# A decoder layer with 32 experts on one core: when the engines read what TensorE has multiplied

## The chip, the cores and the metric

The kernel runs on one core of a Trainium2 chip. The core has five engines with an instruction queue each: TensorE (PE; its weight loads are shown apart as PEld), VectorE (DVE), ScalarE (ACT), GpSimd (POOL) and SyncE (SP), which here issues nearly all transfers; 16 DMA engines move the data. The metric is the time of one execution on the device in microseconds (us); less is better.

## The reference, cut to what matters

One layer: attention in two head groups, then a mixture of experts (each of 512 tokens goes to 4 of 32 experts), then a gated embedding and a last normalisation. The part that the change touches is the mixture:

```
def expert_block(args):            # xs: the tokens of one expert
    e, xs = args
    hh = jnp.dot(xs, w_gu[e]) + b_gu[e]            # 1024 -> 2 x 1024
    glu, lin = jnp.split(hh, 2, axis=-1)
    glu = jnp.minimum(glu, SWIGLU_LIMIT)
    lin = jnp.clip(lin, -SWIGLU_LIMIT, SWIGLU_LIMIT)
    act = glu * jax.nn.sigmoid(SWIGLU_ALPHA * glu) * (lin + 1.0)
    return jnp.dot(act, w_dn[e]) + b_dn[e]         # 1024 -> 1024
...
yr = yb.reshape(n_rows, d) * row_gate[:, None].astype(yb.dtype)
y = jax.ops.segment_sum(yr, row_tok, num_segments=t + 1)[:t]
```

All 32 experts have 8 MB + 4 MB of float32 weights each, and each weight is used once.

## The kernel before

After attention and routing (about the first 345 us) the experts are sorted by how many tokens they have and worked off in 26 **runs**: 20 runs of one expert, with room for 128 tokens down to 72, and 6 runs of two experts with room for 64 tokens each (**pairs**). An expert's weights come in 12 **pieces** of 1 MB: eight "u" pieces (`w_gu`: u0 to u3 the glu half, u4 to u7 the linear half) and four "d" pieces (`w_dn`). A run multiplies its own u pieces and, between them, the d pieces of the run before it, in the order that `phase` writes out (line 48).

Each piece goes through three stages. SP loads it into one of 8 buffers (`RAW`, line 776). Then it is **split**: ACT writes its high half as float16 (`hl`, line 219), DVE what is left of it (line 220), into one of 6 buffers (`HL`). Then TensorE multiplies it in three passes (`mm3`, lines 225 to 227; `down_t`, lines 1357 to 1359). The d pieces of a pair are not split: TensorE reads them as float32 straight from `RAW`. A `RAW` buffer is free again after the split (or after the matmuls that read it), an `HL` buffer after the matmuls. `take(j)` emits the splits up to four pieces ahead of the piece j that it hands out (`AHEAD = 4`, `advance`).

ACT and DVE also read what TensorE has multiplied, out of PSUM banks:

- `gather` (line 1235) picks the tokens of the next run by matmuls with a one-hot matrix `oh`: four banks of `xT` (ACT, line 1250), the gates (DVE, lines 1259 and 1263) and the transposed one-hots `ohT` (ACT, line 1268). It is emitted whole after piece u5.
- `glu_of` after u3 (DVE line 1273, ACT line 1274) and `act_of` after u7 (DVE lines 1280 and 1281), then the split of the result, `acts`.
- `down_t` copies its transposed result `yT` (ACT, `yt`, line 1364) after the last d piece, TensorE turns it back into `y`; `y_out` multiplies it with the gate (ACT `yh`, line 1432; DVE `yl`, line 1433).
- `combine` adds three runs' results to the tokens: eight sums of six matmuls (line 1444), each added to `acc` by DVE (line 1446). `step()` emits one sum after each half of a u piece.

The small matmul results share two PSUM banks (`pg`), the halves of the u product four (`ph`), the d product two (`py`).

What sets the order: the code only emits; a list scheduler then orders each engine's queue by order of emission and by when it thinks that an instruction's operands are there. So an instruction emitted later may stand earlier. `behind(i, j)` (line 135) keeps i behind j on their engine, without a semaphore. Before, nothing in the experts' part is tied in that way. Once built, the order of a queue is fixed.

Of the kernel before, what the change touches and what calls it, by code (L numbers as in the profile page):

```python
# [9 lines left out]
F32 = mybir.dt.float32  # L10
# [45 lines left out]
def hybrid_layer(ctx: ExitStack, tc: tile.TileContext, x, p, positions, w_in, g_attn, g_cq, w_uq, g_ckv,  # L56
# [746 lines left out]
    def advance(upto):  # L803
# [3 lines left out]
        while nsp <= min(upto, len(jobs) - 1):  # L807
            j = jobs[nsp]
            if not native(j):
# [7 lines left out]
                else:  # L817
# [4 lines left out]
                    else:  # L822
                        hl(t[:, :2048], t[:, 2048:], RAW[:, f], SW)
# [401 lines left out]

    def onehots(pos, c, n=1):
# [8 lines left out]
    def gather(oh, gate, c, n=1, parts=True, mid=None):  # L1235

        if parts:
            xT = mp.tile([P, 2, KD, P], F16, name="xT", tag="xT", bufs=2)
        else:
            xT = mp.tile([P, KD, P], F32, name="xTf", tag="xT", bufs=2)  # L1240
        for h in range(2 if parts else 1):
            us = (uhl[h],) if parts else uhl
            for q in range(2):
                ps = pg()
                for k in range(4):
                    for j, u_ in enumerate(us):
                        for i in range(NT):
                            PE.matmul(ps[:, k * c:(k + 1) * c], u_[:, i, (q * 4 + k) * P:(q * 4 + k + 1) * P],  # L1248
                                      oh[:, i, :c], start=i == 0 and j == 0, stop=i == NT - 1 and j == len(us) - 1)
                A.activation((xT[:, h] if parts else xT)[:, q * 4:(q + 1) * 4, :c],  # L1250
                             ps[:, :4 * c].rearrange("p (k c) -> p k c", k=4), AF.Copy, scale=1.0 if parts else SW)
# [5 lines left out]
        gcl = mp.tile([P, 1], F32, name="gcl", bufs=3)  # L1257
        t4 = mp.tile([P, 4], F32, name="t4", bufs=2)
        V.tensor_scalar(t4[:c, :2 * n], ps[:c, 0:2 * n], 1.0 / (SX * SW), None, op0=OP.mult)
        w = c // n  # L1260
        for a in range(n):
            r = slice(a * w, (a + 1) * w)
            V.tensor_tensor(gcl[r], t4[r, a:a + 1], t4[r, n + a:n + a + 1], op=OP.add)
# [3 lines left out]
        ohT = mp.tile([P, SEQ], F16, name="ohT", bufs=5)  # L1267
        A.activation(ohT[:c], tp[:c, :SEQ], AF.Copy)
        return xT, gcl, ohT

    def glu_of(h, n):
        t = mp.tile([P, 512], F32, name="glu", bufs=2)[:, :n]
        V.tensor_scalar(t, h[:, :n], 1.0 / S, 7.0, op0=OP.mult, op1=OP.min)  # L1273
        A.activation(t, t, AF.Gelu_apprx_sigmoid)  # L1274
        return t

    def act_of(h, n, glu):

        t = mp.tile([P, 512], F32, name="ln", bufs=2)[:, :n]
        V.tensor_scalar(t, h[:, :n], 7.0 * S, -7.0 * S, op0=OP.min, op1=OP.max)  # L1280
        V.scalar_tensor_tensor(t, t, S, glu, op0=OP.add, op1=OP.mult)
        return t


    def up(get, put, xT, brow, c, acts):
# [4 lines left out]
        for a in range(2):  # L1290
# [6 lines left out]
            for q in range(4):  # L1297
                slot, w = get(4 * a + q)
                for m in range(2):
# [7 lines left out]
                    step()  # L1307
                put(4 * a + q)
                if q == 3:
                    if a:  # L1310
                        for j, h in enumerate(ps):
                            acts[j] = act_of(h, n, acts[j]).rearrange("p (m c) -> p m c", c=c)
                    else:
                        acts.extend(glu_of(h, n) for h in ps)
                yield

    def act_parts(acts, c):
        t = mp.tile([P, 2, 2, 4, P], F16, name="acts", tag="acts", bufs=1)
        r = [[t[:, j, b, :, :c] for b in range(2)] for j in range(2)]
# [393 lines left out]
```

## Time and profile before

| | us |
|---|---|
| three runs | 1547.34, 1550.41, 1550.46; median 1550.41 |
| the profiled execution | 1548.82 |
| its span, first to last instruction | 1546.7 |
| experts, from the trace | about 345 to 1455 |

The profile lists busy time by engine and stretch, groups of instructions by source line, who waited for whom, and the instructions in order of time. "Busy" of DVE and ACT is the union of their instructions; what is missing to the length of a stretch is idle. The mean granted clock of TensorE is 0.967 of full.

### The profile page before, as it was taken

To read this page: it belongs to the slowest core of one execution; us is meant where nothing else is said; L and a number is where in the kernel's file an instruction comes from. 1 tells how busy PE (TensorE), PEld (TensorE's weight loads), DVE (VectorE), ACT (ScalarE), POOL (GpSimd) and SP (SyncE) were. 2 spreads that over 40 slices of the span, in tenths; PEclk is the share of its full clock that TensorE was granted. 3 is DMA by queue.
4 is the path that set the end of the run, shared out by engine and by line. 5 is a ranking of instruction groups with operands and counts; after the bars stand their busy time and mean duration, and the time that the engine had idled before them with its cause. 6 is when DMAs were issued, how large, how long until landed. Compare 5 with 4: busy or idle time off the path is not lost. (4 is left out here: it accounts for less than half of the span.)

```text
span 1546.7 us, 41528 instructions
## 1 busy us (share of the span) xinstructions
PE 1366.5 (88%) x18126; PEld 981.7 (63%) x18126; DVE 1216.1 (79%) x1356; ACT 1012.6 (65%) x1168; POOL 49.6 (3%) x114
## 2 busy tenths in 40 slices
PE   7999899779989999999999899889889788798587
PEld 4766556475446686467885558868544777674257
DVE  7447876689874899849999669999884898989734
ACT  6458766558463677647777557777853786896534
POOL 2001000310000000000000000000000000000002
PEclk9999999879989999999999999999999999999799
DMA  7122131159999899969999879999996999899711
GB/s 254 41 86 83 56 110 30 54 204 380 355 371 362 320 394 358 345 243 400 404 339 359 328 291 408 383 361 346 341 394 229 375 406 367 285 377 350 282 69 56
DMA packets 124235, 432.81 MB, mean 280 GB/s; under 512 B 7977, under 2 KB 18770, under 8 KB 123986
## 3 DMA queue, kind: packets, MB, share of 16 engines
q1 hardware_dynamic: 123858, 429.85, 75.1%
q8 instruction: 144, 2.36, 0.6%
q14 instruction: 41, 0.34, 0.1%
q10 hardware_dynamic: 192, 0.26, 0.1%
HBM read 427.99 MB, written 2.10 MB: 278 GB/s over the span
## 5 line engine op out<-in xcount | busy, mean ns | idle before, releaser
L220 DVE SCALAR_TENSOR_TENSOR hl<-raw,hl 128x2048 f16<-128x2048 f32 x337 | 762.7, 2286 | 88.6 <-ACT hl L219 87.1
L219 ACT ACTIVATE hl<-raw 128x2048 f16<-128x2048 f32 x337 | 627.0, 1903 | 30.3 <-DMA raw<-in_w_gu_dram 11.1
L227 PE MATMUL hps<-xT,hl 128*128 128x80 f16 (+4 forms) x2560 | 339.2, 208 | 31.3 <-DVE hl L220 29.2
L225 PE MATMUL hps<-xT,hl 128*128 128x80 f16 (+4 forms) x2560 | 351.9, 208 | 3.2 <-ACT hl L219 3.0
L226 PE MATMUL hps<-xT,hl 128*128 128x80 f16 (+4 forms) x2560 | 351.2, 208 | 0.7 <-issue 0.7
L227 PEld LDWEIGHTS <-hl 128*128 128x128 f16 (+1 forms) x2672 | 257.8, 99 | 58.6 <-DVE hl L220 41.6
L225 PEld LDWEIGHTS <-hl 128*128 128x128 f16 (+1 forms) x2672 | 262.0, 99 | 28.2 <-issue 7.9
L226 PEld LDWEIGHTS <-hl 128*128 128x128 f16 (+1 forms) x2672 | 262.3, 99 | 16.9 <-issue 4.5
L1386 PE MATMUL hps<-hl,xT 128*64 128x512 f16 x1152 | 166.7, 404 | 38.8 <-DVE hl L220 30.8
L1386 PEld LDWEIGHTS <-xT 128*64 128x64 f16 x1152 | 77.9, 115 | 112.7 <-issue 73.5
L1358 PE MATMUL yT<-acts,hl 128*128 128x80 f16 (+3 forms) x960 | 122.4, 205 | 7.9 <-DVE acts L220 6.2
L1357 PE MATMUL yT<-acts,hl 128*128 128x80 f16 (+3 forms) x960 | 123.6, 205 | 4.2 <-issue 2.4
L1359 PE MATMUL yT<-acts,hl 128*128 128x80 f16 (+3 forms) x960 | 117.6, 205 | 9.4 <-DVE hl L220 7.8
L1250 ACT ACTIVATE xT<-pg 128x512 f16<-128x512 f32 (+4 forms) x104 | 51.5, 514 | 96.1 <-PE pg L1248 86.7
L1386 PE MATMUL y<-raw,actT 128*64 128x512 f32 x384 | 108.2, 603 | 0.0
L1359 PEld LDWEIGHTS <-hl 128*128 128x128 f16 x960 | 93.1, 100 | 20.5 <-DVE hl L220 11.2
L1357 PEld LDWEIGHTS <-hl 128*128 128x128 f16 x960 | 94.1, 100 | 11.4 <-issue 8.5
L1444 PE MATMUL pg<-yh,ohT 128*128 128x512 f16 (+4 forms) x208 | 81.9, 395 | 19.6 <-DVE acc L1446 13.2
L1358 PEld LDWEIGHTS <-hl 128*128 128x128 f16 x960 | 94.8, 100 | 3.2 <-issue 2.2
L1444 PE MATMUL pg<-yl,ohT 128*128 128x512 f16 (+4 forms) x208 | 81.4, 394 | 0.7 <-DVE yl L1433 0.6
L1444 PEld LDWEIGHTS <-ohT 128*128 128x128 f16 (+4 forms) x416 | 38.2, 100 | 67.9 <-issue 39.1
L1274 ACT ACTIVATE glu<-glu 128x512 f32<-128x512 f32 (+4 forms) x52 | 27.6, 550 | 70.3 <-DVE glu L1273 70.2
(376 smaller groups left out, 2339.1 us busy)
## 6 DMA issues: line engine op xcount, KB each, us to landing
raw<-in_w_gu_dram SPq DMA_DIRECT2D x256, 1024.0 KB, 8.4
raw<-in_w_dn_dram SPq DMA_DIRECT2D x128, 1024.0 KB, 8.7
raw<-in_w_in_dram SPq DMA_DIRECT2D x2, 2048.0 KB
raw<-in_w_o_dram SPq DMA_DIRECT2D x2, 2048.0 KB
raw<-in_w_ple_gate_dram SPq DMA_DIRECT2D x4, 1024.0 KB
acc<-in_x_dram SPq DMA_DIRECT2D x4, 512.0 KB, 3.6
raw<-in_w_in_dram SPq DMA_DIRECT2D x4, 512.0 KB, 7.1
out_dram<-acc SPq DMA_DIRECT2D x8, 256.0 KB, 2.4
```

What stands on the lines that cost most here:

```text
L219: later["hl"] = (A.activation(hi, src, AF.Copy, scale=scale), V.scalar_tensor_tensor(lo, src, scale, hi, op0=OP.mult, op1=OP.subtract))
L220: V.scalar_tensor_tensor(lo, src, scale, hi, op0=OP.mult, op1=OP.subtract))
L225: PE.matmul(ps, ah, bh, start=first, stop=False, skip_group_check=True)
L226: PE.matmul(ps, ah, bl, start=False, stop=False, skip_group_check=True)
L227: PE.matmul(ps, al, bh, start=False, stop=last, skip_group_check=True)
L1250: A.activation((xT[:, h] if parts else xT)[:, q * 4:(q + 1) * 4, :c], ps[:, :4 * c].rearrange("p (k c) -> p k c", k=4), AF.Copy, scale=1.0 ...
L1274: A.activation(t, t, AF.Gelu_apprx_sigmoid)
L1357: PE.matmul(o[f], w[0][:, m, r], ah, start=first and f % 4 == 0, stop=False, skip_group_check=True)
L1358: PE.matmul(o[f], w[0][:, m, r], al, start=False, stop=False, skip_group_check=True)
L1359: PE.matmul(o[f], w[1][:, m, r], ah, start=False, stop=last, skip_group_check=True)
L1386: PE.matmul(ps[n][E2[e]], xT[:, k, E2[e]] if whole else xT[:, a, k, E2[e]], (ws[e][1] if whole else ws[e][1][b])[:, m, c], start=not opene ...
L1444: PE.matmul(ps, ohT[:c, i * P:(i + 1) * P], y_[:c, n * 512:(n + 1) * 512], start=e == 0 and q == 0, stop=e == last and q == 1)
```

## The change

Five things change, all in the experts' part; every engine has as many instructions as before.

1. Results of TensorE are no longer read where they are emitted. The reading is put on a list by `after`, together with the last split emitted by then, and `flush` emits it, each instruction tied `behind` that split on its own engine. For the products of weights (`glus`, `acts_of`, `act_parts`, `yt`) `flush` follows at once after the piece; for gather, gates, sums and `y_out` it follows after the next piece.
2. `gather` is a generator of three steps (first half of `xT`, second half, gates and `ohT`), one step after each piece from d2 on.
3. `step` deals out two sums after each piece, d pieces too, instead of one after each half of a u piece, where no gather step is due.
4. The first d piece stands after u2 instead of u1, the second after u3.
5. The head and the tail get the calls of `flush` that this needs.

```diff
-    return [u[0], u[1], d[0], u[2], d[1], u[3], u[4], d[2], u[5], d[3], u[6], u[7]] if u and d else u + d
+    return [u[0], u[1], u[2], d[0], u[3], d[1], u[4], d[2], u[5], d[3], u[6], u[7]] if u and d else u + d
...
-                        hl(t[:, :2048], t[:, 2048:], RAW[:, f], SW)
+                        later["split"] = hl(t[:, :2048], t[:, 2048:], RAW[:, f], SW)
...
+    due = []
+
+    def after(f):
+        due.append((f, later.get("split")))
+
+    def flush():
+        while due:
+            f, sp = due.pop(0)
+            for i in f():
+                if sp is not None:
+                    behind(i, sp[0 if i.ins.engine == sp[0].ins.engine else 1])
+
+    def inline(steps):
+        for _ in steps:
+            flush()
...
+        def bank(us, o, q, scale):
+            ps = pg()
+            for k in range(4):
+                for j, u_ in enumerate(us):
+                    for i in range(NT):
+                        PE.matmul(ps[:, k * c:(k + 1) * c], u_[:, i, (q * 4 + k) * P:(q * 4 + k + 1) * P],
+                                  oh[:, i, :c], start=i == 0 and j == 0, stop=i == NT - 1 and j == len(us) - 1)
+            after(lambda: [A.activation(o[:, q * 4:(q + 1) * 4, :c], ps[:, :4 * c].rearrange("p (k c) -> p k c", k=4),
+                                        AF.Copy, scale=scale)])
...
             if mid is not None and not h:
+                flush()
                 mid()
+            yield
...
+        def gates():
+            t4 = mp.tile([P, 4], F32, name="t4", bufs=2)
+            yield V.tensor_scalar(t4[:c, :2 * n], ps[:c, 0:2 * n], 1.0 / (SX * SW), None, op0=OP.mult)
+            for a in range(n):
+                q = slice(a * w, (a + 1) * w)
+                yield V.tensor_tensor(gcl[q], t4[q, a:a + 1], t4[q, n + a:n + a + 1], op=OP.add)
+
+        after(gates)
...
+        after(lambda: [A.activation(ohT[:c], tp[:c, :SEQ], AF.Copy)])
+        yield
+
+    def glus(ps, n, r):
+
+        def first():
+            for h in ps:
+                r.append(mp.tile([P, 512], F32, name="glu", bufs=2)[:, :n])
+                yield V.tensor_scalar(r[-1], h[:, :n], 1.0 / S, 7.0, op0=OP.mult, op1=OP.min)
+            after(lambda: [A.activation(t, t, AF.Gelu_apprx_sigmoid) for t in r])
+
+        after(first)
+
+    def acts_of(ps, n, r, then):
+
+        def f():
+            for j, h in enumerate(ps):
+                t = mp.tile([P, 512], F32, name="ln", bufs=2)[:, :n]
+                yield V.tensor_scalar(t, h[:, :n], 7.0 * S, -7.0 * S, op0=OP.min, op1=OP.max)
+                yield V.scalar_tensor_tensor(t, t, S, r[j], op0=OP.add, op1=OP.mult)
+                r[j] = t
+            then()
+
+        after(f)
...
-                    step()
                 put(4 * a + q)
                 if q == 3:
                     if a:
-                        for j, h in enumerate(ps):
-                            acts[j] = act_of(h, n, acts[j]).rearrange("p (m c) -> p m c", c=c)
+                        acts_of(ps, n, acts, lambda: then(acts, c))
                     else:
-                        acts.extend(glu_of(h, n) for h in ps)
+                        glus(ps, n, acts)
                 yield
...
-                for n in range(2):
-                    A.activation(yt[n], ps[n][:, :4 * c], AF.Copy)
+                after(lambda: [A.activation(yt[n], ps[n][:, :4 * c], AF.Copy) for n in range(2)])
...
-                V.scalar_tensor_tensor(acc[:, i, n * 512:(n + 1) * 512], ps, 1.0 / SX,
-                                       acc[:, i, n * 512:(n + 1) * 512], op0=OP.mult, op1=OP.add)
+                a_ = acc[:, i, n * 512:(n + 1) * 512]
+                after(lambda ps=ps, a_=a_: [V.scalar_tensor_tensor(a_, ps, 1.0 / SX, a_, op0=OP.mult, op1=OP.add)])
                 yield 1
 
     sums = []
 
-    def step(n=1):
-
+    def step(n=2):
...
+        def f():
+            for n in range(2):
+                s_ = slice(n * 512, (n + 1) * 512)
+                yield A.activation(yh[:c, s_], y[n][:c], AF.Copy, scale=gcl[:c])
+                yield V.scalar_tensor_tensor(yl[:c, s_], y[n][:c], gcl[:c], yh[:c, s_], op0=OP.mult, op1=OP.subtract)
+
+        after(f)
         return yh, yl
...
             if u_ == "u":
                 next(g_up)
+                flush()
                 if q == 0 and turned_:
                     prev[2] = turn2(prev[2])
+                    continue
                 if q == 3:
                     at(ns_, 1)
+                if q == 4:
+                    at(ns_, 2)
+                    flush()
+                    step(99)
+                    if ns_ < LAST:
+                        nxt = []
+                        g_prep = prep(RUNS[ns_ + 1], nxt)
+                    continue
                 if q == 6 and g_down is not None:
                     next(g_down)
                     ended()
                     g_down = None
-                if q == 5:
-                    at(ns_, 2)
-                    if ns_ < LAST:
-                        step(99)
-                        nxt = prep(RUNS[ns_ + 1])
+                if g_prep is not None:
+                    next(g_prep, None)
+                else:
+                    step()
                 continue
             if q == 0:
                 ps_ = RUNS[prev[0]]
                 if not now:
                     prev[2] = turn2(prev[2])
+                    flush()
                 g_down = (down2 if len(ps_) > 1 else down if prev[1] == P else down_t)(
                     *access(ps_), prev[2], *(() if len(ps_) > 1 else (prev[1],)), prev[5])
             next(g_down)
-            if q == 3 and prev[5]:
+            flush()
+            if q == 3 and prev[5] and len(prev[5]) == 2 and (len(ps_) > 1 or prev[1] == P):
                 ended()
                 g_down = None
-        if now and len(us) == 1:
-            acts = act_parts(acts, c)
+            if g_prep is not None:
+                next(g_prep, None)
+            else:
+                step()
```

Two places in the queues. The first is **ACT** in a run of 80 tokens late in the expert part, from its reading of the glu half (`glu`) to that of the result (`yh`); `hl<-raw` is the split of a piece, `xT` and `ohT` the gather for the next run, `yt` the copy of the transposed result. Before:

```order
L1268 ACTIVATE ohT_17955<-ohT_ps_17950 80x512
L219 ACTIVATE hl_83<-raw_82 128x2048 x4
L1274 ACTIVATE glu_17697<-glu_17697 128x320
L1274 ACTIVATE glu_17700<-glu_17700 128x320
L219 ACTIVATE hl_83<-raw_82 128x2048 x3
L1364 ACTIVATE yt_18008<-yT_17491 128x320
L1364 ACTIVATE yt_18009<-yT_17492 128x320
L219 ACTIVATE hl_83<-raw_82 128x2048
L1432 ACTIVATE yh_18073<-y_18063,gcl_16552 80x512
L1432 ACTIVATE yh_18073<-y_18064,gcl_16552 80x512
```

And with the change, the same run:

```order
L1305 ACTIVATE glu_17648<-glu_17648 128x320
L219 ACTIVATE hl_83<-raw_82 128x2048 x2
L1270 ACTIVATE xT_17817<-pg_17820 128x4x80
L1270 ACTIVATE xT_17817<-pg_17837 128x4x80
L219 ACTIVATE hl_83<-raw_82 128x2048
L1270 ACTIVATE xT_17817<-pg_17907 128x4x80
L1270 ACTIVATE xT_17817<-pg_17924 128x4x80
L219 ACTIVATE hl_83<-raw_82 128x2048
L1401 ACTIVATE yt_17992<-yT_17542 128x320
L1401 ACTIVATE yt_17993<-yT_17543 128x320
L1296 ACTIVATE ohT_17819<-ohT_ps_18003 80x512
L219 ACTIVATE hl_83<-raw_82 128x2048
```

The gather, which stood ahead of the glu half, now stands between glu and `yt`, one step to a piece, and `yt` has four splits between itself and glu where it had three; glu itself has moved back too, so that both now follow the splits of some four pieces beyond the one whose product they read (counted over both queues: `yt` 2.0 pieces in the median before and 4.2 now, DVE's glu 1.2 and 4.0, `xT` 2.5 and 4.0).

The second is **DVE** in a run of 96 tokens that closes a group of three, from `yl` (the last result of the group) on; `acc<-pg` adds a sum, `ln` and `acts` are the linear half and the result of the activation. Before:

```order
L1433 SCALAR_TENSOR_TENSOR yl_14426<-y_14416,gcl_12756,yh_14425 96x512
L1446 SCALAR_TENSOR_TENSOR acc_84<-pg_14458,acc_84 128x512
L220 SCALAR_TENSOR_TENSOR hl_83<-raw_82,hl_83 128x2048
L1446 SCALAR_TENSOR_TENSOR acc_84<-pg_14490,acc_84 128x512
L220 SCALAR_TENSOR_TENSOR hl_83<-raw_82,hl_83 128x2048
L1280 TENSOR_SCALAR ln_14498<-hps_14055 128x320
L1280 TENSOR_SCALAR ln_14501<-hps_14056 128x320
L220 SCALAR_TENSOR_TENSOR hl_83<-raw_82,hl_83 128x2048
```

And with the change:

```order
L1472 SCALAR_TENSOR_TENSOR yl_14426<-y_14416,gcl_12628,yh_14425 96x512
L220 SCALAR_TENSOR_TENSOR hl_83<-raw_82,hl_83 128x2048
L1314 TENSOR_SCALAR ln_14482<-hps_14055 128x320
L1314 TENSOR_SCALAR ln_14485<-hps_14056 128x320
L1315 SCALAR_TENSOR_TENSOR ln_14482<-ln_14482,glu_13998 128x320
L1315 SCALAR_TENSOR_TENSOR ln_14485<-ln_14485,glu_14000 128x320
L220 SCALAR_TENSOR_TENSOR hl_83<-raw_82,hl_83 128x2048
L220 SCALAR_TENSOR_TENSOR acts_14488<-ln_14482,acts_14488 128x4x80
L220 SCALAR_TENSOR_TENSOR acts_14488<-ln_14485,acts_14488 128x4x80
L220 SCALAR_TENSOR_TENSOR hl_83<-raw_82,hl_83 128x2048
L1488 SCALAR_TENSOR_TENSOR acc_84<-pg_14564,acc_84 128x512
L1488 SCALAR_TENSOR_TENSOR acc_84<-pg_14571,acc_84 128x512
```

The eight sums began right behind `yl`, one to a split; now the first two stand three splits later, and all eight follow in four pairs with one split between two pairs.

## Rows read from the trace of the kernel before

**Rows 1.** The page: span; busy us, share of span, instructions of each engine

```profile
span 1546.7 us, 41528 instructions
PE 1366.5 (88%) x18126; PEld 981.7 (63%) x18126; DVE 1216.1 (79%) x1356; ACT 1012.6 (65%) x1168; POOL 49.6 (3%) x114
```

**Rows 2.** Stretches, us from start: busy us by engine, clock, DMA share, GB/s

```profile
400.00:520.00 120.00, 109.10 (x952) 61.99 (x952) 74.92 (x65) 54.86 (x47) 0.00 (x0) 0.96 0.91 339
640.00:700.00 60.00, 59.19 (x645) 38.80 (x645) 36.74 (x32) 27.16 (x23) 0.00 (x0) 0.97 0.76 276
860.00:910.00 50.00, 45.43 (x495) 26.10 (x495) 25.04 (x22) 20.78 (x20) 0.00 (x0) 1.00 0.78 282
1150.00:1200.00 50.00, 45.38 (x539) 25.77 (x536) 25.29 (x26) 17.29 (x18) 0.00 (x0) 1.00 0.67 247
```

**Rows 3.** The same view, the other expert stretches after 700 us

```profile
700.00:780.00 80.00, 76.90 (x1294) 66.74 (x1292) 75.26 (x57) 61.75 (x51) 0.00 (x0) 1.00 1.02 402
780.00:860.00 80.00, 72.32 (x1055) 54.10 (x1053) 74.38 (x61) 61.31 (x53) 0.00 (x0) 0.98 0.98 350
915.00:990.00 75.00, 69.95 (x1489) 65.23 (x1487) 69.78 (x57) 57.29 (x54) 0.00 (x0) 1.00 1.02 403
990.00:1150.00 160.00, 134.75 (x2441) 105.34 (x2440) 149.04 (x119) 123.49 (x105) 0.00 (x0) 0.97 0.99 361
1210.00:1290.00 80.00, 64.74 (x1454) 56.67 (x1451) 75.87 (x63) 64.06 (x54) 0.00 (x0) 0.98 1.02 407
1290.00:1450.00 160.00, 131.03 (x2331) 97.69 (x2328) 146.01 (x126) 124.56 (x134) 0.00 (x0) 0.98 0.95 342
```

**Rows 4.** DVE's longest wait in 700:860, 910:1150, 1200:1450: us, times, longest

```profile
DVE hl L220 <- ACT hl L219: 8.3, 8, 2.7
DVE hl L220 <- ACT hl L219: 13.0, 11, 2.7
DVE hl L220 <- ACT hl L219: 14.6, 14, 1.9
```

**Rows 5.** ACT in order of time, 1222 to 1235: start, us [idle <-releaser]

```profile
1223.79 5.50 ACT L219 ACTIVATE hl<-raw 128x2048 f16<-128x2048 f32 x3
1231.62 0.87 ACT L1364 ACTIVATE yt<-yT 128x320 f32<-128x320 f32 x2 [2.34 <-PE yT L1359]
1232.39 1.90 ACT L219 ACTIVATE hl<-raw 128x2048 f16<-128x2048 f32 x1
```

**Rows 6.** DVE at the same place

```profile
1223.31 9.10 DVE L220 SCALAR_TENSOR_TENSOR hl<-raw,hl 128x2048 f16<-128x2048 f32 x4
1234.32 2.29 DVE L220 SCALAR_TENSOR_TENSOR hl<-raw,hl 128x2048 f16<-128x2048 f32 x1 [1.91 <-ACT hl L219]
```

**Rows 7.** Waits of ACT in 910:1150

```profile
ACT glu L1274 <- DVE glu L1273: 18.9, 7, 6.2
ACT yt L1364 <- PE yT L1359: 10.2, 5, 3.3
ACT xT L1250 <- PE pg L1248: 6.0, 6, 2.5
ACT hl L219 <- DMA raw<-in_w_dn_dram: 2.5, 2, 1.9
```

**Rows 8.** Groups, 450:1430: xcount | busy us, mean ns | idle before

```profile
L220 DVE SCALAR_TENSOR_TENSOR hl<-raw,hl 128x2048 f16<-128x2048 f32 x294 | 664.7, 2284 | 79.3 <-ACT hl L219 78.0
L1250 ACT ACTIVATE xT<-pg 128x512 f16<-128x512 f32 x28 | 16.2, 593 | 20.7 <-PE pg L1248 20.7
```

**Rows 9.** TensorE in order of time: two matmuls of one sum

```profile
1288.12 0.38 PE L1444 MATMUL pg<-yh,ohT 128*128 128x512 f16 x1
1288.34 0.38 PE L1444 MATMUL pg<-yl,ohT 128*128 128x512 f16 x1
```

**Rows 10.** TensorE's wait for the gather's copies, 420:1380

```profile
PE pg L1248 <- ACT xT L1250: 1.6, 4, 0.6
```

**Rows 11.** The page, transfers: count, KB each, median us to landing

```profile
raw<-in_w_gu_dram SPq DMA_DIRECT2D x256, 1024.0 KB, 8.4
```

More of the change, by code (lines that the diff above doesn't have):

```diff
@@ L1240, in gather @@
             xT = mp.tile([P, KD, P], F32, name="xTf", tag="xT", bufs=2)
+        gcl = mp.tile([P, 1], F32, name="gcl", bufs=3)
+        ohT = mp.tile([P, SEQ], F16, name="ohT", bufs=5)
+        r.extend((xT, gcl, ohT))
+        def bank(us, o, q, scale):
[7 more added lines that the diff above has]
+                                        AF.Copy, scale=scale)])
         for h in range(2 if parts else 1):
-            us = (uhl[h],) if parts else uhl
             for q in range(2):
[L1244 to L1251, printed above, removed]
+                bank((uhl[h],) if parts else uhl, xT[:, h] if parts else xT, q, 1.0 if parts else SW)
             if mid is not None and not h:
+                flush()
                 mid()
+            yield
         ps = pg()
@@ L1266, in gather, with up @@
             PE.transpose(tp[:c, i * P:(i + 1) * P], oh[:, i, :c], ident)
[L1267 to L1285, printed above, removed]
+        after(lambda: [A.activation(ohT[:c], tp[:c, :SEQ], AF.Copy)])
[16 more added lines that the diff above has]
+        after(f)
+    def up(get, put, xT, brow, c, acts, then):
         per = 512 // c if c <= 64 else 4
@@ L1318, in act_parts, with act_whole @@
         t = mp.tile([P, 2, 2, 4, P], F16, name="acts", tag="acts", bufs=1)
-        r = [[t[:, j, b, :, :c] for b in range(2)] for j in range(2)]
-        for j in range(2):
-            hl(*r[j], acts[j], SX / S)
-        return r
+        whole = [a.rearrange("p (m c) -> p m c", c=c) for a in acts]
+        acts[:] = [[t[:, j, b, :, :c] for b in range(2)] for j in range(2)]
+        after(lambda: [i for a, w in zip(acts, whole) for i in hl(*a, w, SX / S)])
+    def act_whole(acts, c):
+        acts[:] = [a.rearrange("p (m c) -> p m c", c=c) for a in acts]
     def ybanks(name="y"):
@@ L1402, in up2 @@
                 pair_mm(ps, xT, 2 * q, 4 * a + q, get, put, True)
[L1403 removed]
                 if q == 3:
                     if a:
[L1406 removed]
+                        acts_of(ps, 512, acts, lambda: None)
                     else:
[L1408 removed]
+                        glus(ps, 512, acts)
                 yield
@@ L1498, in prep @@
             between()
-        return gather(oh, lambda i: X_[:, i, 0:2, s_:s_ + n], n * CAPS[s_], n, mid=mid)
+        return gather(oh, lambda i: X_[:, i, 0:2, s_:s_ + n], n * CAPS[s_], n, r, mid=mid)
     def at(ns_, k):
@@ L1602, in hybrid_layer @@
     SY.dma_start(gfb, g_final.rearrange("(o d) -> o d", o=1).to_broadcast([P, D]))
+    later.pop("split")
     overflow()
     advance(len(jobs) - 1)
+    later.pop("split", None)
     ov = out.rearrange("(i p) d -> p i d", p=P)
```

65 lines of the change are left out of this document (38 added, 27 removed).

## The prediction, made before the changed kernel had run

> **What bounds the kernel now.** I read the page's first lines, then the stretches, then DVE's waits, then one wait in order of time. On the page PE is busy 88% of the span and DVE 79% [rows 1]; neither is the bound everywhere, so the stretches decide. There the expert part falls into two kinds. In the first kind, 280 us in four stretches, PE is busy 259.1 us and DVE 162.0: the splits are done ahead and wait for room, and TensorE sets the pace [rows 2]. They are the runs of 128 tokens and those behind a pair. In the other kind, 635 us after 700 us, DVE is busy 590.3 us and PE 549.7 [rows 3]: here the split of a piece on DVE, 2.284 us each [rows 8], with DVE's other work around it, sets the pace. Transfers are the third candidate. Their share reads about 1 nearly everywhere, but the rate tells more: in 700 to 780, 915 to 990 and 1210 to 1290 it is 402 to 407 GB/s, in the other three stretches 342 to 361 [rows 3]. A piece is 1 MB [rows 11]: at 405 GB/s 2.59 us, at 356 GB/s 2.95 us. So in the three low-rate stretches DVE asks for less than the queue has shown it can bring, and in the three high-rate ones (where the buffers fill again after a pair) there is little to spare.
>
> DVE's idle time in the stretches that it paces is 4.7 + 5.6 + 5.2 + 11.0 + 4.1 + 14.0 = 44.6 us [rows 3]. Most of it has one name: DVE waits for ACT's half of a split, 8.3 + 13.0 + 14.6 = 35.9 us over slightly longer stretches [rows 4]. Why ACT is late is seen near 1230 us: ACT has done three splits and then stands 2.34 us until TensorE has made `yT`; only then come `yt` and the next split, so DVE, after four splits on end, stands 1.91 us [rows 5, 6]. In 910 to 1150 ACT stood so five times for `yt`, 10.2 us, and 6.0 us for `xT`; its largest wait, 18.9 us for DVE's `glu`, is the harmless kind, ACT being ahead of DVE [rows 7].
>
> At this place the Trainium skill (Perfetto Trace Analysis, Optimization Strategy) has another reading: the same gap again and again on the engine that should be saturated can mean that SBUF or PSUM has no room for the next tile. The trace does not agree: the gap of rows 6 ends with a split on ACT, which stood on a product and not on a buffer. By that rule the new order would move no time; I keep it as a rival.
>
> **The change part by part.** No engine gets an instruction more or less, so nothing is to be priced but waits.
>
> *Readers of products tied behind the last split* (list items 1 and 2). Before, `yt` stood two pieces' splits behind its product, glu 1.2, `xT` 2.5; now about four. When DVE sets the pace, TensorE eats a split piece soon after it is made, so a product four pieces back is long there, and ACT no longer stands on `yT` or `pg`. What goes with it is DVE's wait for ACT. Bounds: below, nothing or a loss (the rivals); above, all 44.6 us. In the three high-rate stretches, 4.7 + 5.2 + 4.1 = 14.0 us, I count nothing, as a transfer of 2.59 us is late next. Of the other 30.6 us I take two thirds, 20.4 us: by rows 7 about as much of ACT's waiting is for DVE as for PE, and the lead of `actT` (the turned activations of a pair) does not grow.
>
> *What stands behind the tied instructions.* Behind a tied glu on DVE stands the next split, and for that TensorE waits; but the tied one now finds its operand there and only costs its own time, which it cost before. In the stretches that TensorE paces, ACT now may wait at a tied reader for TensorE, with the next split behind it; but four split pieces lie ready by then, and TensorE works on them while ACT waits for the product of an earlier one, so TensorE loses nothing. I count 0 there; above, TensorE's own idle time, 10.9 + 0.8 + 4.6 + 4.6 = 20.9 us [rows 2], could shrink too.
>
> *Sums two at a time, gather one step per piece* (items 2 and 3). TensorE's work is the same. A sum is six matmuls, 0.22 us apart [rows 9]: two are 2.6 us a piece, over four pieces where they were spread over five. DVE's additions are the same number. Count 0 as long as the two `pg` banks come free in time; the price if not is the second rival's.
>
> *d0 behind u2* (item 4). `acts` gets one piece more before TensorE asks for it; behind a pair, 2 MB that are not split are asked for a piece later and held so. Bounds: one transfer of 2.59 us either way for each of six pairs, plus or minus 15.5 us. I take 0: it falls where TensorE is busy 259 of 280 us [rows 2] and its work does not change.
>
> *Head and tail* (item 5): the attention before 345 us and the end after 1455 us keep their order; 0.
>
> Sum: -20.4 us. The profiled execution took 1548.82 us, 2.1 us more than its span [rows 1]; 1548.82 - 20.4 = 1528.4. It was 1.6 us below the median of the three runs, 1550.41; I give the time on their scale: **1530 us**.
>
> **The rivals.**
>
> *A larger gain.* If also the high-rate stretches' 14.0 us and the last third go, and half of TensorE's 20.9 us: 44.6 + 10.5 = 55.1, that is 1493.7, on the runs' scale 1495 us. For it: ACT, the first reader of a landed piece, waited for one 2.5 us in 240 us [rows 7]. Against: 402 to 407 GB/s is the most that any stretch shows.
>
> *No change.* The gaps return elsewhere, as the third stage (landing, or a free `HL` buffer) was late next all along: 1550 us. For it: transfers read a share near 1 in all six stretches, and 20.4 us of the 400 us of the low-rate stretches are 5%, so a piece every 2.80 us is asked for. Against: the low-rate stretches have brought pieces in 2.95 us while the high-rate ones take 2.59. The skill's rule above would come out here.
>
> *Slower: TensorE stands on PSUM banks.* The gather's second half, the gates and the next two sums need the two `pg` banks, and these are now emptied only behind the split of a piece four ahead. TensorE's queue goes no further meanwhile. Price: in a group of three runs three pairs of sums stand behind a first pair, each up to one split, 2.284 us [rows 8]; 26 runs make some eight groups, 8 x 3 x 2.284 = 55 us. In the seven gathers of 128 tokens (28 copies, four each [rows 8]), where TensorE sets the pace, two steps each stand behind a split on ACT, 1.90 us [rows 5], and two copies of 0.593 us: 7 x 2 x 3.1 = 43 us. Together 98 us if all is exposed. The gain is used up from 20.4/98, 21%, on; with a third exposed it is 33 - 20 = 12 us more, 1561 us, on the runs' scale 1563 us. For it: six `HL` buffers, of which four are now always ahead of the reader, leave two for unevenness. Against: the wait is 1.6 us in all today [rows 10], and TensorE idles 85 us in the stretches that DVE paces [rows 3], where such a wait costs nothing until it outgrows that.
>
> That matmuls start and complete in program order is also what the Trainium skill says (PSUM — Partial Sum Buffer, Engine vs sequencer instructions): one matmul without a bank holds all behind it, those whose weights are ready too. No row of before shows it at work beyond rows 10; by it the whole 98 us would be exposed wherever TensorE paces.
>
> *The change does not do what it says.* The scheduler could have undone the ties; the two orders show that it has not, except for `actT` and a part of the sums. That leaves a smaller gain, 5 us, 1545 us.
>
> **How the numbers follow.** Forecast with its own range of 1516 to 1543: 0.57. Larger gain: 0.07. Smaller gain: 0.06. No change: 0.12. Slower: 0.18. Faster by over 0.2% (3.1 us, about what a measurement of this kernel can tell): 0.57 + 0.07 + 0.06 = 0.70; within it 0.12; slower 0.18. The range that holds 8 in 10 leaves out about half of the larger gain and half of the slower case: 1506 to 1560. It takes in the whole of the unpriced places on the good side (44.6 us) and 10 us of the bad.
>
> **What would show it.** Right: `yt <- PE yT` and `xT <- PE pg` nearly vanish from ACT's waits, DVE's wait for ACT's `hl` after 700 us falls from 36 us to about 12, and the rate in the low-rate stretches rises from 351 GB/s in the mean to about 370 (351/0.95). TensorE's `hps <- DVE hl` waits may stay. Wrong: TensorE's waits for `xT`, `yt` or `acc` grow to tens of us (the slower rival), ACT's waits for landings grow by what the others lose (no change), or the four stretches of rows 2 change in length by more than 10 us, which I count at nothing.

## The result and the profile after

The changed kernel takes **1513.23 us** (median of four runs, 1512.45 to 1515.55); the kernel before took 1550.43 beside it. The ratio is 0.9763, 95% interval 0.9743 to 0.9784: 37 us faster. Forecast were 1530 us, with a range of 1506 to 1560. The direction was right; the forecast gain of 20.4 us was a little over half of the real one, and the larger part of the gain goes back to places for which the prediction counted nothing.

The page of the changed kernel, which answers to [rows 1]; the execution took 1515.55 us:

```profile
span 1513.7 us, 41574 instructions
PE 1354.5 (89%) x18126; PEld 985.1 (65%) x18126; DVE 1214.4 (80%) x1356; ACT 1009.7 (67%) x1168; POOL 49.5 (3%) x114
```

The work is the same: 18126 matmuls, DVE's busy time within 2 us (TensorE's, in which the ends of matmuls are modelled, is 12 us less). The span is 33 us shorter, so idle time went. To see where, stretches of equal work have to be laid beside each other, since everything shifts. The 384 pieces of weights serve as marks: SP issues them (line 776) in nearly the same order in both kernels, and the time at which the n-th is issued is in the trace. The stretches below run from piece 60 to 80, 112 to 144, 192 to 208 and 288 to 304 (four stretches behind pairs, where unsplit d pieces are multiplied; those of the first and the last pair are left out), and then 144 to 192, 208 to 288 and 304 to 380 (what lies between and after). Columns as in [rows 2]. The kernel before:

```profile
464.40:530.30 65.90, 63.87 (x707) 42.83 (x704) 38.85 (x35) 30.96 (x26) 0.00 (x0) 1.00 0.88 330
625.60:723.40 97.80, 95.25 (x1045) 62.09 (x1044) 71.50 (x56) 56.07 (x46) 0.00 (x0) 0.98 0.86 319
865.60:920.20 54.60, 52.31 (x640) 32.41 (x640) 29.64 (x28) 22.45 (x21) 0.00 (x0) 1.00 0.76 270
1152.90:1210.20 57.30, 51.30 (x709) 32.91 (x707) 30.58 (x30) 23.35 (x25) 0.00 (x0) 0.97 0.69 255
723.40:865.60 142.20, 129.48 (x2039) 104.25 (x2035) 132.43 (x103) 108.86 (x91) 0.00 (x0) 0.99 1.00 374
920.20:1152.90 232.70, 202.41 (x3865) 168.06 (x3863) 216.51 (x172) 178.72 (x157) 0.00 (x0) 0.98 1.00 375
1210.20:1452.80 242.60, 195.57 (x3773) 154.16 (x3771) 224.48 (x194) 189.71 (x189) 0.00 (x0) 0.97 0.98 364
```

The changed kernel, the same pieces:

```profile
464.90:524.80 59.90, 59.90 (x713) 42.92 (x713) 35.47 (x30) 29.25 (x25) 0.00 (x0) 1.00 1.01 390
619.40:713.30 93.90, 90.36 (x1030) 60.91 (x1029) 71.28 (x57) 55.60 (x46) 0.00 (x0) 1.00 0.91 353
851.60:898.40 46.80, 45.12 (x600) 29.43 (x598) 26.09 (x19) 22.06 (x21) 0.00 (x0) 1.00 0.94 353
1125.80:1176.70 50.90, 48.76 (x672) 30.22 (x670) 30.77 (x28) 22.39 (x22) 0.00 (x0) 1.00 0.88 334
713.30:851.60 138.30, 132.01 (x2115) 108.20 (x2113) 132.08 (x103) 110.71 (x97) 0.00 (x0) 0.99 0.99 373
898.40:1125.80 227.40, 197.56 (x3878) 168.66 (x3876) 217.83 (x178) 177.97 (x158) 0.00 (x0) 0.99 0.99 369
1176.70:1418.20 241.50, 198.23 (x3833) 160.27 (x3830) 226.18 (x201) 188.12 (x189) 0.00 (x0) 0.94 0.98 362
```

The four pair stretches went from 275.6 us to 251.5, 24.1 less; the three between from 617.5 to 607.2, 10.3 less. Read the two last columns: between the pairs the transfers' share was 0.98 to 1.00 and stays there. Behind the pairs it was 0.88, 0.86, 0.76 and 0.69. Length times what is missing to 1 gives 7.9 + 13.7 + 13.1 + 17.8 = 52.5 us in which no weights came; after, it is 16.8 (a share above 1 counted as it stands). TensorE was busy 263 of 276 us there before, so nothing on its row shows the loss.

These marks are issues, which run ahead of TensorE. Marked by TensorE itself, the time shows elsewhere. From its last matmul on one pair's unsplit pieces (`y<-raw` in the trace) to its first on the next pair's, the five stretches add up to 878 us before and 852 after; on the unsplit pieces themselves (pairs two to six, first to last such matmul) it spends 152 and 144 us. In e3 below, the changed kernel without ties, the two are 881 and 139 us, and in e7, with ties at the pairs and right behind them alone, 850 and 143. So the transfers stand while TensorE is at a pair, and what the ties save there TensorE gets back after it.

How the transfers come to stand, in the kernel before, behind the pair near 890 us. ACT in order of time (start, duration, idle before and its releaser):

```profile
891.61 1.89 ACT L219 ACTIVATE hl<-raw 128x2048 f16<-128x2048 f32 x1
896.28 0.59 ACT L1268 ACTIVATE ohT<-ohT_ps 96x512 f16<-96x512 f16 x1 [2.78 <-PE ohT_ps L1266]
905.10 0.69 ACT L1432 ACTIVATE yh<-y,gcl 128x512 f16<-128x512 f32 x1 [8.22 <-PE y L1386]
905.96 0.69 ACT L1432 ACTIVATE yh<-y,gcl 128x512 f16<-128x512 f32 x1 [0.17 <-PE y L1386]
906.54 7.30 ACT L219 ACTIVATE hl<-raw 128x2048 f16<-128x2048 f32 x4
```

SP's issues at the same place:

```profile
890.24 9.14 SPq L776 DMA_DIRECT2D raw<-in_w_gu_dram  x4
910.85 0.37 SPq L776 DMA_DIRECT2D raw<-in_w_dn_dram  x1
```

`yh` reads the pair's result `y`, for which TensorE has to finish the last d pieces. It stands in ACT's queue ahead of four splits, which then follow on end; so these wait up to 8.22 us, and with them DVE, which stands 6.84 us at `yl`. `RAW` buffers come free only after a split: the last of the four issues ends at 899.38 and SP issues nothing more before 910.85, 11.5 us. SP's waits from 865 to 920 us (us, times, longest) all have this name:

```profile
SPq L776 <- DVE hl L220: 45.7, 10, 11.2
```

The same place in the changed kernel, ACT:

```profile
891.41 3.70 ACT L219 ACTIVATE hl<-raw 128x2048 f16<-128x2048 f32 x2
895.01 1.26 ACT L1471 ACTIVATE yh<-y,gcl 128x512 f16<-128x512 f32 x2
896.15 0.59 ACT L1296 ACTIVATE ohT<-ohT_ps 96x512 f16<-96x512 f16 x1
896.62 5.51 ACT L219 ACTIVATE hl<-raw 128x2048 f16<-128x2048 f32 x3
```

Now the splits stand first and `yh` finds `y` there. Five of ACT's waits (us, times, longest) over the whole expert part, before, 400 to 1452 us:

```profile
ACT xT L1250 <- PE pg L1248: 78.6, 33, 9.2
ACT glu L1274 <- DVE glu L1273: 69.6, 24, 11.4
ACT yh L1432 <- PE y L1386: 30.5, 9, 8.9
ACT yt L1364 <- PE yT L1359: 25.0, 11, 3.3
ACT hl L219 <- DMA raw<-in_w_gu_dram: 11.1, 9, 4.1
```

and after, 400 to 1420 us:

```profile
ACT glu L1305 <- DVE glu L1304: 105.8, 22, 10.8
ACT hl L219 <- DMA raw<-in_w_gu_dram: 49.2, 19, 6.0
ACT xT L1270 <- PE pg L1268: 37.1, 27, 5.4
ACT yh L1471 <- PE y L1406: 6.2, 5, 2.8
ACT yt L1401 <- PE yT L1397: 0.7, 1, 0.7
```

ACT's waits for TensorE have shrunk, and its wait for `w_gu` pieces to land has grown from 11.1 to 49.2 us: it now stands more often at the split, ready when a piece lands. The `yh` row after is that of single experts (L1406); for a pair's `y` there is no wait left in it. (The last pair's `yh`, later than both lists, waits some 14 us in either kernel.) Other waits stay: 37.1 us at `xT`, 33.3 at `actT` (47.3 before), and the longest, ACT's for DVE's half of `glu`, which grew from 69.6 to 105.8 us. What these cost was not taken apart. By stretch the 49.2 us are 16.2 at the first pairs (400 to 465 us), 31.1 in the four pair stretches (12.7 + 4.6 + 8.1 + 5.7) and 1.8 in the three between: behind the pairs the transfers are now late last, between them they are not.

### The profile page after: what moved, and what is told of

It reads as the page before. It is cut to its first block, busy times and chain, and to the rows that moved or that the text cites. A ratio compares the mean times of both kernels' runs of the same rounds, so it can differ in the third digit from the quotient of the medians.

```text
span 1513.7 us, 41574 instructions
## 1 busy us (share of the span) xinstructions
PE 1354.5 (89%) x18126; PEld 985.1 (65%) x18126; DVE 1214.4 (80%) x1356; ACT 1009.7 (67%) x1168; POOL 49.5 (3%) x114
## 5 line engine op out<-in xcount | busy, mean ns | idle before, releaser
L219 ACT ACTIVATE hl<-raw 128x2048 f16<-128x2048 f32 x337 | 627.1, 1902 | 80.8 <-DMA raw<-in_w_gu_dram 49.2
L227 PE MATMUL hps<-xT,hl 128*128 128x80 f16 (+4 forms) x2560 | 346.6, 209 | 31.9 <-DVE hl L220 19.6
L225 PEld LDWEIGHTS <-hl 128*128 128x128 f16 (+1 forms) x2672 | 263.3, 99 | 27.5 <-issue 11.1
L1423 PE MATMUL hps<-hl,xT 128*64 128x512 f16 x1152 | 161.9, 397 | 27.8 <-DVE hl L220 21.5
L1423 PEld LDWEIGHTS <-xT 128*64 128x64 f16 x1152 | 75.4, 113 | 95.5 <-issue 51.5
L1395 PE MATMUL yT<-acts,hl 128*128 128x80 f16 (+3 forms) x960 | 123.6, 207 | 3.8 <-ACT acts L219 2.1
L1396 PE MATMUL yT<-acts,hl 128*128 128x80 f16 (+3 forms) x960 | 122.9, 207 | 2.0 <-issue 1.3
L1397 PE MATMUL yT<-acts,hl 128*128 128x80 f16 (+3 forms) x960 | 120.8, 207 | 0.7 <-DVE hl L220 0.6
L1395 PEld LDWEIGHTS <-hl 128*128 128x128 f16 x960 | 95.6, 101 | 10.8 <-issue 6.3
L1485 PE MATMUL pg<-yh,ohT 128*128 128x512 f16 (+4 forms) x208 | 81.5, 393 | 19.4 <-DVE acc L1488 10.2
L1397 PEld LDWEIGHTS <-hl 128*128 128x128 f16 x960 | 95.6, 101 | 4.6 <-issue 2.2
L1396 PEld LDWEIGHTS <-hl 128*128 128x128 f16 x960 | 96.3, 101 | 0.9
L1270 ACT ACTIVATE xT<-pg 128x512 f16<-128x512 f32 (+4 forms) x104 | 50.6, 511 | 44.1 <-PE pg L1268 42.6
```

The lines of the kernel that those rows point to most:

```text
L219: later["hl"] = (A.activation(hi, src, AF.Copy, scale=scale), V.scalar_tensor_tensor(lo, src, scale, hi, op0=OP.mult, op1=OP.subtract))
L225: PE.matmul(ps, ah, bh, start=first, stop=False, skip_group_check=True)
L227: PE.matmul(ps, al, bh, start=False, stop=last, skip_group_check=True)
L1270: after(lambda: [A.activation(o[:, q * 4:(q + 1) * 4, :c], ps[:, :4 * c].rearrange("p (k c) -> p k c", k=4), AF.Copy, scale=scale)])
L1395: PE.matmul(o[f], w[0][:, m, r], ah, start=first and f % 4 == 0, stop=False, skip_group_check=True)
L1396: PE.matmul(o[f], w[0][:, m, r], al, start=False, stop=False, skip_group_check=True)
```

## The experiments

Two readings were to be told apart. **S** (steady), the prediction's: the ties free the stretches that DVE paces. **P** (pairs): they keep the splits, and through them the transfers, going while TensorE works on a pair's unsplit pieces. In the table "gain" is (1 - ratio) x 1550 us, "pair stretches" and "between" are the lengths of the four and the three stretches above, by the same pieces, and "no transfer" is the time without transfers in the four, worked out as above from the shares of each run's trace. The lengths come from one profiled execution of each kernel, which lies up to some 5 us from the median of its runs (e7: 1513.33 us against 1518.46), so a few us between two lengths say little.

| kernel | ratio, 95% interval | gain | pair stretches | no transfer | between |
|---|---|---|---|---|---|
| before | 1 | 0 | 275.6 | 52.5 | 617.5 |
| changed | 0.9763, 0.9743 to 0.9784 | 36.7 | 251.5 | 16.8 | 607.2 |
| e1 old order of d0 | 0.9721, 0.9701 to 0.9741 | 43.2 | 242.1 | 6.5 | 610.9 |
| e3 no ties | 0.9967, 0.9952 to 0.9983 | 5.1 | 271.0 | 51.5 | 611.8 |
| e4 no delay | 0.9758, 0.9735 to 0.9782 | 37.5 | 251.3 | 15.3 | 612.6 |
| e5 gather in a lump | 0.9848, 0.9816 to 0.9879 | 23.6 | 255.0 | 16.0 | 617.0 |
| e6 before + ties | 0.9860, 0.9823 to 0.9898 | 21.7 | 247.2 | 14.8 | 617.4 |
| e7 ties at pairs | 0.9794, 0.9775 to 0.9813 | 31.9 | 252.9 | 13.0 | 604.4 |
| e8 ties elsewhere | 0.9932, 0.9911 to 0.9953 | 10.5 | 268.0 | 50.2 | 604.8 |
| e9 old order, no delay | 0.9705, 0.9682 to 0.9728 | 45.7 | 242.2 | 7.1 | 613.4 |
| e10 ties on yh, yl only | 0.9943, 0.9924 to 0.9962 | 8.8 | 262.7 | 34.9 | 612.4 |
| e11 ties on the gather only | 0.9898, 0.9872 to 0.9924 | 15.8 | 263.1 | 41.9 | 610.1 |
| e12 e1 + tie on oh | 0.9764, 0.9739 to 0.9790 | 36.6 | 239.9 | 9.3 | 620.8 |
| e14 ties on yh, yl and gather | 0.9822, 0.9804 to 0.9839 | 27.6 | 255.1 | 28.9 | 608.8 |

**e3, the ties alone taken out.**

```diff
-                if sp is not None:
+                if False:
                     behind(i, sp[0 if i.ins.engine == sp[0].ins.engine else 1])
```

> The changed kernel with the ties alone taken out: the same instructions, emitted a piece later as changed, and dealt out as changed, but the scheduler is free to put a reader ahead of the last split. Theory S: the ties make the gain, it goes: 1540 to 1550 us, lost evenly in the stretches that DVE paces. Theory P with the dealt gather as its cause: 1513 to 1522, the three steps behind the pairs stay.

Measured: 5 us left of 37, 1545.22 us. The ties are worth 31.6 us; later emission and dealing out without them almost nothing, since the scheduler puts the readers ahead again. The time is the one that S gave (1540 to 1550 us), and P with the dealt gather as its cause (1513 to 1522) is out. But S had the loss spread evenly, and it is not: 19.5 us of it lies in the pair stretches and 4.6 between. What is left of P is that the ties work at the pairs. ACT, DVE and the transfers behind the pair near 890 us, first ACT, then DVE, then a stretch (columns as above):

```profile
890.23 1.90 ACT L219 ACTIVATE hl<-raw 128x2048 f16<-128x2048 f32 x1
905.72 0.69 ACT L1471 ACTIVATE yh<-y,gcl 128x512 f16<-128x512 f32 x1 [13.59 <-PE y L1423]
907.16 7.30 ACT L219 ACTIVATE hl<-raw 128x2048 f16<-128x2048 f32 x4
```

```profile
883.31 1.07 DVE L1304 TENSOR_SCALAR glu<-hps 128x384 f32<-128x384 f32 x2 [7.61 <-PE hps L227]
```

```profile
880.00:890.00 10.00, 10.00 (x111) 5.78 (x112) 3.78 (x5) 4.40 (x7) 0.00 (x0) 1.00 0.05 18
```

ACT stands 13.59 us for `y`, ahead of four splits again. A little earlier ACT stands 5.78 us at `xT` and then DVE 7.61 us at `glu`, and the transfers run at 18 GB/s for 10 us, with TensorE busy 10.00 of them. That is how the loss hides.

**e7 and e8, ties only at pairs, and only elsewhere.**

```diff
+            pair_ = len(us) > 1 or prev is not None and len(RUNS[prev[0]]) > 1
+            later["tie"] = pair_          # e8: not pair_
...
-                if sp is not None:
+                if sp is not None and later["tie"]:
```

> The changed kernel with ties only in the runs of a pair of experts and in the run behind each pair (11 of 26 runs), none in the others. Theory P (the gain is made where the unsplit d pieces of a pair are multiplied): at least 25 of the 32 us that the ties are worth stay, 1513 to 1520. Theory S (each run with ties gains the same, in the stretches that DVE paces): 11/26 of 32 stay, 1531 us.

> The counterpart: ties only in the 15 runs that are not a pair and do not follow one. Theory P: at most 7 us of the 32 stay, 1538 to 1545. Theory S: 15/26 of 32 stay, 1527 us.

Measured: of the 31.6 us 26.8 stay with the ties at pairs and 5.4 with the ties elsewhere; the two add up. P as expected; S would have had 13 and 18. The stretch from piece 192 to 208 in e7 and, below it, in e8:

```profile
852.90:899.70 46.80, 45.13 (x600) 29.45 (x598) 26.09 (x19) 22.05 (x21) 0.00 (x0) 1.00 0.98 365
```

```profile
866.10:921.70 55.60, 51.27 (x629) 33.82 (x629) 27.42 (x24) 21.12 (x21) 0.00 (x0) 0.94 0.72 265
```

The same 16 pieces in 46.8 us as in the changed kernel, or in 55.6 as before, with the transfers at 0.98 or 0.72.

**e10, e11 and e14, one kind of tie or two.** In e3's place, only `y_out` (e10), only the gather's copies, gates and `ohT` (e11), or both (e14) are tied:

```diff
-    def after(f):
-        due.append((f, later.get("split")))
+    def after(f, tied=False):
+        due.append((f, later.get("split") if tied else None))
...
+            after(..., True)     # of the kinds named
```

> The changed kernel with one kind of tie only: the readers of an expert's output y (yh on ScalarE, yl on VectorE). Without any tie yh stands ahead of the next splits on ScalarE and waits 32 us in all for TensorE's y, up to 13.6 us at a pair, and it took 1545 us. Theory Y (yh, wanted long before the unsplit d pieces are through, is what stops the splits): 15 to 25 of the 32 us come back, 1520 to 1530. Theory X (the gather's copies are it): at most 8 us, 1537 to 1545.

> The changed kernel with ties only on what reads the gather's products (xT and ohT on ScalarE, the gates on VectorE). Without any tie xT waits 71 us in all for TensorE, with all ties 37. Theory X: 15 to 25 of the 32 us come back, 1520 to 1530. Theory Y: at most 8 us, 1537 to 1545. If both kinds share it, each stopping the splits in the other's absence: both kernels at 1535 to 1545.

> The changed kernel with two kinds of tie: the readers of y (yh, yl) and of the gather's products (xT, gates, ohT); glu, acts, actT, yt and acc are not tied. Alone they gave 5 and 12 of the 32 us. Independent: 17 of 32, 1527 us. If a stop taken away at one reader is taken up by the next on the same engine, the two together give more than their sum, 25 or more: 1513 to 1520. If actT and glu stop the splits in their place: 1530 to 1535.

Measured, over the 5.1 us without ties: 3.7 us with `yh` alone, 10.7 with the gather alone, 22.5 with both. My theory Y, that `yh` is the main stop, is wrong; the gather's copies weigh more, yet less than theory X had. (1532.80 us in e11 and 1522.52 in e14 lie in none of the ranges expected.) ACT's waits in e10, and below in e11, 400 to 1440 us:

```profile
ACT xT L1270 <- PE pg L1268: 68.3, 36, 9.6
ACT actT L1454 <- PE pg L1453: 40.3, 7, 13.6
```

```profile
ACT yh L1471 <- PE y L1423: 40.7, 8, 16.3
ACT actT L1454 <- PE pg L1453: 25.2, 6, 6.6
```

In e10 no wait of a pair's `yh` is left, but `actT` waits longer, 40.3 us where it is 29.2 in e3; in e11 `xT` waits 5.6 us in all, but `yh` 40.7 us where it is 32.1 in e3. A stop taken away at one reader is in part taken up by the next in the same queue. The two together gave 8 us more than their sum, with an uncertainty of 6 us (the four intervals added in squares): it points that way and doesn't settle it. The 9 us from both to all ties belong to `glu`, `acts`, `actT`, `yt` and `acc`; they were not taken apart.

**e1 and e9, the order of the d pieces and the delay.**

```diff
-    return [u[0], u[1], u[2], d[0], u[3], d[1], u[4], ...
+    return [u[0], u[1], d[0], u[2], d[1], u[3], u[4], ...
```

> The changed kernel (1513 us) with one part undone: d0 stands behind u1 again, as before; delay, ties, gather and sums as changed. Theory S (steady): the ties free the stretches that DVE paces, and the order is worth nothing: 1513 +- 4 us, and the weight pieces are issued as early as in the changed kernel all along. Theory P (pairs): the gain is made where a pair's d pieces, which are not split, are multiplied, since splits and transfers go on there; it can come from the order (a piece more before acts is wanted), then two thirds of 37 us return: 1535 to 1545, lost in three steps behind the pairs at pieces 128 to 132, 200 to 204 and 296 to 304; or from the gather and the ties, then 1513 to 1518.

> The changed kernel with d0 behind u1 as before and without the delay of a piece; ties, dealt gather and sums as changed. The first alone gave 1506.6 us, the second 1513.4. If the two are independent: 1503 to 1509. If acts, wanted a piece earlier by the old order, needs the delay out of its way: 1500 to 1504.

Measured: with the old order 1506.62 us, 6.5 us *faster* than the changed kernel (the intervals of the two ratios, each against its own runs of before, just fail to overlap). None of my theories had that. Its pair stretches are 9.4 us shorter, and the transfers' share there is 0.95 to 1.00; from piece 192 to 208:

```profile
848.80:892.10 43.30, 42.54 (x600) 28.68 (x598) 26.09 (x20) 22.30 (x22) 0.00 (x0) 1.00 0.99 376
```

That is 43.3 us against 46.8. That the new order puts a pair's first d pieces a place later in the transfers too, and holds their buffers so, would fit, but was not tried apart. e9, with the delay gone as well, is the fastest kernel at 1506.09 us; it can't be told from e1, and lies where two independent parts were expected (1503 to 1509 us). Both beat the kernel before and the changed one.

**e4, no delay.**

```diff
     def after(f):
         due.append((f, later.get("split")))
+        flush()
```

> The changed kernel without the delay: each reader is emitted at once behind its product, and still tied behind the last split. The last split is four pieces ahead of the product either way. Theory S: the lead in splits is what counts and it stays about the same: 1513 to 1520 us. If the one piece of delay is what keeps ACT from standing on TensorE: 1530 to 1550. Theory P with the dealt gather: 1513 to 1522.

Measured: 1513.37 us, the same as the changed kernel. Emitting readers a piece later is worth nothing once they are tied; the ties put them behind the splits.

**e5, the gather in a lump, and e6, the kernel before with the ties alone.** In e5 the steps of the gather all follow u5:

```diff
-                if g_prep is not None:
-                    next(g_prep, None)
+                if q == 5 and ns_ < LAST:
+                    nxt = []
+                    inline(prep(RUNS[ns_ + 1], nxt))
```

> The changed kernel with the gather not dealt out: all of the next run's gather is emitted behind u5, as before, its copies still tied behind the last split. Theory S: 1513 to 1520 us. Theory P with the gather as its cause (four copies in a row on ACT with no split between, while TensorE is on native pieces): the three steps behind the pairs, 11 to 13, 7 and 11 to 13 us, go: 1538 to 1548.

In e6 each reader in the kernel before is tied where it was emitted:

```diff
-        A.activation(t, t, AF.Gelu_apprx_sigmoid)
+        tie(A.activation(t, t, AF.Gelu_apprx_sigmoid))
```

> The kernel before with the ties alone: every reader of an expert product is emitted where it was and tied behind the split made last; gather in one lump, sums one at a time, the old order, no delay. Without the ties the changed kernel had lost all but 5 us of its 37. Theory T (the ties alone are the change, and the gather costs a little when it is a lump): 1512 to 1525 us. Theory C (ties help only with readers dealt out, since tied in a lump they make ACT stand): 1535 to 1550.

Measured: e5 loses 13 us, e6 has 21.7 of the 36.7 us (its runs spread from 1521.82 to 1534.09). Neither fits one theory alone. The pair stretches are near those of the changed kernel (255.0 and 247.2 us): the ties do that, lump or not. But between the pairs both stand at 617 us, like the kernel before; the kernels with the dealt gather stand at 604 to 613 there, tied or not (e12, at 620.8, apart). One of ACT's waits in e5 and one of DVE's, at the gates, 400 to 1440 us:

```profile
ACT xT L1270 <- PE pg L1268: 61.1, 32, 8.4
DVE t L1287 <- PE pg L1282: 34.9, 18, 8.0
```

and DVE's at the gates in the changed kernel:

```profile
DVE t L1287 <- PE pg L1282: 0.5, 1, 0.5
```

With the ties on, the copies of `xT` still wait 61.1 us for TensorE where the dealt gather has 37.1, and DVE waits 34.9 us at the gates instead of 0.5: tied in a lump, the gather's readers make both engines stand. So the 24 us behind the pairs are the ties'. The 10 us between them are not there without the dealt gather; but with it and without the ties (e3) only 5.7 of them are, so they seem to need both. With one execution of each this is not settled.

**e12, one tie more.** In e1 DVE waits 20.7 us at the one-hot matrix `oh`, which the change left untied:

```diff
+        if later.get("split") is not None:
+            behind(o_, later["split"][1])      # o_ writes oh
```

> The kernel with the old order of d0 (1506.6 us, all else as changed) and one tie more: the one-hot oh on VectorE, which no list item touched, is tied behind the last split too. There VectorE waited 20.7 us in 10 times for the transposes that free oh's buffer. If splits are held up by it as by the other readers: 1497 to 1503 us. If the gap only moves to landings, for which ScalarE waits 66 us there: 1505 to 1508. If TensorE then waits for oh: 1508 to 1515.

Measured: 6 us slower than e1, 1512.61 us (the two intervals just touch). DVE's and ACT's waits, 400 to 1440 us, in e1:

```profile
DVE hl L220 <- ACT hl L219: 80.4, 63, 7.8
DVE oh L1247 <- PE ohT_ps L1295: 20.7, 10, 3.5
...
ACT xT L1270 <- PE pg L1268: 23.3, 24, 3.3
```

and in e12:

```profile
DVE hl L220 <- ACT hl L219: 107.7, 75, 6.5
...
ACT xT L1272 <- PE pg L1270: 52.9, 35, 5.8
```

The wait for `oh` has gone, but `oh` is not a reader that can wait; it feeds the gather. TensorE now waits 5.1 us for it (in e1 not at all), the copies of `xT` wait 29.6 us more for their product, and DVE waits for ACT 27.3 us more. The gap came back two engines on.

## Why the prediction was right, and where it was wrong

**The cause was right, its place only by a part.** That ACT and DVE stand at products with splits queued behind, and that the ties end this, is shown by e3: without them 5 of 37 us are left. e7 and e8 show that five sixths of what the ties give comes from the runs of a pair and those behind one, 11 of the 26.

**The step that failed** is the one on what stands behind the tied instructions: "four split pieces lie ready by then, and TensorE works on them ... so TensorE loses nothing. I count 0 there". That TensorE loses next to nothing there holds: by its own marks it spends 144 us on the unsplit pieces with the ties, 139 without them and 152 before. But the step asks only what TensorE pays at that place, and leaves out what the old order cost later. There, a split that waits keeps a `RAW` buffer, SP then issues nothing (11.5 us at one pair), and the transfers that were missed were not made up: the stretches that follow were no shorter for it (617.5 us before, 607.2 after), with DVE busy 573 of the 617 us. That they could not be made up is argued from this; no run tried it. [Rows 2] had the loss in their share column (0.91, 0.76, 0.78 and 0.67), beside TensorE's 259 of 280 us, from which I argued. What the runs show in place of the 0: ties at the pairs and behind them alone are worth 26.8 of the 31.6 us (e7). The prediction's own sign of failure, a change of the four stretches by over 10 us, came true by the marks of issues (24.1 us); by TensorE's marks that time shows between the pairs.

**That the time fell into the range** of 1506 to 1560 us was in part luck. Its good end was made of DVE's 44.6 us of idle time, of which 13 us went (below); the rest of the gain came by way of the step counted at 0.

**The term of 20.4 us** in the stretches that DVE paces measured about 10.3 by the marks of issues (all three stretches between, the high-rate ones included). The signs foreseen for it did come: `yt <- PE yT` went from 25.0 to 0.7 us, and DVE's wait for ACT in these three stretches fell from 34.2 (8.3 + 13.0 + 12.9) to 15.6 us (3.4 + 2.5 + 9.7), against about 12 expected. Only a little over half of that became time: DVE now waits 13.2 us for `oh` there, and its idle time fell from 44.1 to 31.1 us. The rate, over these whole stretches, did not rise (374, 375 and 364 GB/s before, 373, 369 and 362 after). And in e5 and e6 even these 10 us are missing without the dealt gather, which I had counted at 0. Two readings on the way are a little off and change nothing: at the 351 GB/s that the low-rate rows average a piece takes 2.99 us, not 2.95, and in the stretch of [rows 7] ACT waited 1.9 us for `w_gu` pieces besides the 2.5 for `w_dn`.

**d0 behind u2**, taken as 0 between bounds of plus and minus 15.5 us, costs 6.5 us (e1). The reason given for 0, that TensorE is busy there, is the one that failed above.

**The rivals.** The slower one did not decide: TensorE's waits for a `pg` bank to be read grew from 1.8 us (`xT` 1.6, `acc` 0.2) to 10.2 (`acc`), against a price of 98 if all were exposed. "No change" had landings late next; they are, but only behind the pairs, as shown above, where the transfers stood before. The larger gain was about as near in size as the forecast (1513 lies half way between 1530 and 1495), but not in its source: it added the high-rate stretches and TensorE's idle time, not transfers that stood. That the ties do what they say is seen in the ACT rows above.

**The Trainium skill's reading** of a recurring gap (Perfetto Trace Analysis, Optimization Strategy: it can mean that SBUF or PSUM has no room for the next tile) is half borne out at the pairs: the load does wait for an SBUF buffer, 11.5 us at one pair, but the buffer is held by a split that waits for a product, and ties without any more room shortened it: SP's longest wait for a split there is 7.8 us in the changed kernel against 11.2, and the transfers' share 0.94 against 0.76.

## What to carry to other kernels

In an in-order queue, put what feeds others (splits, one-hots) first and what reads a product late behind it; tie it, if a scheduler orders the queue, since emitting it later did next to nothing here (e3, e4). Readers that are tied should be dealt out, not stand in a lump (e5). Do this above all where the busiest engine is fully busy on work that the other stages need not prepare: a stop of loads and splits is invisible there and is paid for in the next stretch. So look for stretches in which the transfers' share falls below that of their neighbours, even if TensorE is at 100%, and count what is missing to 1 as time that a later stretch may have to pay.

## What was not expected of the hardware

The transfers' share reads 0.98 to 1.02 at rates anywhere from 350 to 407 GB/s [rows 3], so a share of 1 does not say how much is carried. A share below 1 does tell something: over the 14 kernels in the table the time without transfers in the four pair stretches falls from 52.5 to 6.5 us as the gain rises from 0 to 43.2 (e1; 7.1 us at 45.7 in e9). The two don't go together everywhere: they part by over 6 us in e5, e6, e7, e10 and e12, which gained 7 to 16 us less than transfers came back, and in e8, which gained 8 more. In e5, e6 and e12 the stretches between are 10 to 14 us longer than in the changed kernel; in the other three, why is open.
